# Out-projection of a linear-attention layer: seven feature blocks of the products first, the transposes one token block behind, the first feed-forward pair in column halves

## The chip, the core and the metric

One Trainium2 chip, one of its cores. The metric is the device time of one execution in microseconds (us); lower is better. TensorE (PE) multiplies, VectorE (DVE), ScalarE (ACT) and GpSimd (POOL) work on rows, and SP issues most of the loads. Line numbers such as L173 are those of the kernel before.

## What is computed

512 tokens of 1024 features go through two blocks and a third layer behind them. The change lies in the first block, between its linear attention (eight groups of 128 features) and its feed-forward. Cut to what matters:

```python
def rwkv7_out(y, ...):
    ...
    return ((yn + bonus) * gate) @ w_o            # yn: y normalised per head of 64; w_o: 1024 x 1024

def first_block(x, ...):                          # i = 0
    ...
    h = x * (1.0 + sc1) + sh1
    y = rwkv7_mixer(h, ...)                       # ends in rwkv7_out
    x = layer_norm(DN_ALPHA * x + gt1 * y, ln_g[i, 0], ln_b[i, 0])
    x = layer_norm(DN_ALPHA * x + gt2 * channel_mixer(x * (1.0 + sc2) + sh2), ln_g[i, 1], ln_b[i, 1])

def swiglu(h, w1, w3, w2):                        # the channel_mixer here, 2816 hidden features
    return (jax.nn.silu(h @ w1) * (h @ w3)) @ w2
```

The vectors sh1, sc1, gt1, sh2, sc2 and gt2 are products of a conditioning vector with a table `ada_w` (6144 columns for each block).

## The kernel before

Every large product is made three times: a matrix is split into a high part that TensorE takes exactly (a cast on ScalarE, L167) and a low part, the rest (a subtraction on VectorE, L168), and `mm3` (L173) sums high x high, high x low and low x high.

**Attention tail.** `tail(f)` normalises the attention output of feature group f, adds the bonus, multiplies by the gate and writes the 128 features x 512 tokens to DRAM, `ygd[f]`. Three of its row operations are on GpSimd (L909, L913 and the product with `rs`, L924).

**Out-projection** (in `body`, L2113 to L2142). The eight pieces of `ygd` are loaded into `xres`, split into the high and low part of y (`y3`, two of the three buffers of the pool `act`), and then `x` is loaded over them into `xres`. After that the loads and splits of `w_o` stand in the code. The loop goes over four blocks of 128 tokens; for each, two halves of 512 output features, each of 8 feature blocks x 3 = 24 products of 512 columns into one bank of PSUM, and `resid_add` (L1314 to L1318, two VectorE operations of 128 x 512: product with the gate, sum with `xres`). Then `norm_tail` normalises the block's rows and brings them into feature order: statistics on VectorE, three small steps on GpSimd (L1136 to L1138), the scaling on ScalarE (L1139), two row operations on GpSimd that write `xres` for later (L1148, L1149), eight transposes on TensorE (L1162), eight scaled copies out of PSUM, `u` (ScalarE L1169, VectorE L1171 in turns), and the split into the high and low part `hT` (L167, L168 "act<-u"). `hT` is allocated at the first block: its high part gets the third `act` buffer, its low part that of y's high part, so that the low part's first write waits for y's last reader.

**Feed-forward.** `phase_ffn` goes over pairs of 128 hidden features; `glu` makes for each feature 24 products with w1 and 24 with w3 over all 512 tokens. Weights come by `load_w` (L155) in pieces of 1 MB through the pool `w` (four buffers) and are split in `k.part`. After each feature the generator `side` takes a step of `ada_sum`: eight loads of `ada_w` (L283, 256 KB each, three slots) and a running sum over them on VectorE (L288, or ScalarE L285 and GpSimd L286 for a second table), and three steps later a sum over partitions on TensorE (L274). These slots and sums lie in `free`, the next `act` buffer, that of y's low part:

```python
free = tok()
nc.gpsimd.memset(free[:, 3], 0.0)
side = (x for g in (k.ada_sum(free, psp, sp, 0, a["ada_w"][1], a["ada_b"][1], "1", False), ...
block, room = phase_ffn(k, hT, xres, gate0, psp, sp, gp, act, side)
```

The order in which each engine takes its instructions is fixed at build time by a scheduler; each engine and each load queue then works in order.

Of the kernel before, what the change touches and what calls it, by code (L numbers as in the profile page):

```python
# [18 lines left out]
NT = 512  # L19
NCX = 256  # L20
NA = NT + NCX
KB = 8
# [98 lines left out]
def at(t, *ix):  # L121

    return t[0][ix], t[1][ix]
# [181 lines left out]
def phase_rwkv(k, tables, tables2, modulate, yg):  # L305
# [223 lines left out]
    with ExitStack() as eb:  # L529
# [372 lines left out]
        def tail(f):  # L902

            st = fst[f]
            y3 = st["ysb"]
            vtok = k.t(tp1, [128, 4, 128], tag="vtok")
            nc.sync.dma_start(out=vtok, in_=vd[0:NT, f * 128:(f + 1) * 128].rearrange("(b p) n -> p b n", p=128))
            vh = vtok.rearrange("p b (h v) -> p (b h) v", h=2)
            nc.gpsimd.tensor_tensor(out=vh, in0=vh, in1=st["cf"][:, :, None].to_broadcast([128, 8, 64]), op=OP.mult)  # L909
# [3 lines left out]
            nc.gpsimd.tensor_tensor(out=y3, in0=y3, in1=mean[:, :, None].to_broadcast([128, 8, 64]), op=OP.subtract)  # L913
# [10 lines left out]
            nc.gpsimd.tensor_tensor(out=y3, in0=y3, in1=rs[:, :, None].to_broadcast([128, 8, 64]), op=OP.mult)  # L924
# [217 lines left out]
def norm_tail(k, sp, psp, tb, xres, gbc, bbc, hT, scol, bcol):  # L1142
# [7 lines left out]
    if hT is not None:  # L1150
        to_feature(k, sp, psp, xh, hT, slice(tb * 128, (tb + 1) * 128), scol, bcol)
# [49 lines left out]
def glu(k, psp, sp, xT, n, w1, w3, g):  # L1201
# [3 lines left out]
    for i in range(w1.shape[2] // 128):  # L1205
        pss = []
        for w in (w1, w3):
# [52 lines left out]
def phase_ffn(k, hT, xres, gate2, psp, sp, gp, act, side):  # L1260
# [4 lines left out]
    for f0, f1 in FCH:  # L1265
# [5 lines left out]
        for f in range(f0, f1, 2):  # L1271
# [7 lines left out]
            with tc.issue_after(k.sums.ins) if k.sums is not None else nullcontext():  # L1279
                glu(k, psp, sp, hT, NT, w1, w3, out)  # L1280
# [774 lines left out]
def body(tc, a, out):  # L2055
    nc = tc.nc
    with ExitStack() as es:
# [45 lines left out]
        with ExitStack() as e1:  # L2103
# [9 lines left out]
            with tc.tile_pool(reuse_waits="tile", name="wo3", bufs=5) as wo3:  # L2113
                y3 = feat()

                yg = xres.rearrange("p t d -> p (t d)").rearrange("p (f n) -> p f n", f=KB)
                for f in range(KB):
                    nc.sync.dma_start(out=yg[:, f, :], in_=ygd[f])
                for f in range(KB):
                    k.part_to(*at(y3, ALL, f), yg[:, f, :])  # L2120
                nc.sync.dma_start(out=xres, in_=a["x"][0].rearrange("(t p) d -> p t d", p=128))
# [4 lines left out]
                hT = None  # L2126
                for tb in range(4):
                    for hf in range(2):
                        ps = k.t(psp, [128, 512], tag="mm")
                        for kk in range(KB):  # L2130
                            k.mm3(ps, at(y3, ALL, kk, slice(tb * 128, (tb + 1) * 128)), at(ws[hf * 4 + kk // 2], ALL, kk % 2), kk == 0, kk == KB - 1)
                        resid_add(k, sp, tb, hf, ps, gate, xres)
                    hT = hT or feat()
# [139 lines left out]
```

## Time and profile before

| | |
|---|---|
| median of 3 runs | 3027.36 us (3026.72 to 3030.48) |
| the profiled execution | 3030.04 us; span of the core 3028.3 us |
| mean granted TensorE clock | 0.903 |
| TensorE busy | 2658.0 us (88%) |
| VectorE, ScalarE, GpSimd busy | 1716.0 us (57%), 1333.8 us (44%), 825.0 us (27%) |
| memory read and written | 419.34 MB and 55.39 MB, 157 GB/s over the span |

Busy shares are means over some thirty different stages and say little about one of them. The places that the change touches lie between 1040 and 1330 us of the span.

### The profile page before, as it was taken

How to read it: one execution, taken by the hardware profiler on the slowest of the kernel's cores; microseconds unless marked ns; L12 is line 12 of the kernel's file. 1: busy time of each engine (PE TensorE's matmuls, PEld its weight loads, DVE VectorE, ACT ScalarE, POOL GpSimd, SP SyncE). 2: the span in 40 equal slices, each digit the busy share in tenths (PEclk: the TensorE clock that was granted, in tenths of full speed). 3: DMA queues.
4: the chain of work that ended last, by engine and by line, in shares of the span. 5: the costliest groups of instructions: out<-in, count | busy, mean ns of one | idle time of the engine just before them, and what ended most of it. 6: DMA issues, size and time to landing. Idle time of an engine off the chain costs nothing. (4 is left out here: it accounts for less than half of the span.)

```text
span 3028.3 us, 47973 instructions
## 1 busy us (share of the span) xinstructions
PE 2658.0 (88%) x18816; PEld 2001.1 (66%) x18816; DVE 1716.0 (57%) x2526; ACT 1333.8 (44%) x2338; POOL 825.0 (27%) x908
## 2 busy tenths in 40 slices
PE   5878788898898756989998999999958989989999
PEld 3666577677776545768776666455547845778887
DVE  5865566756655436664446323456676367554544
ACT  5644555555554423215452322345544377442422
POOL 2453434534534321016654300000023200112120
PEclk8976888997887867989998999999979989999999
DMA  7572344544543535666541877778662212122321
GB/s 257 182 222 66 96 125 142 181 137 129 172 133 95 186 129 165 222 189 212 186 150 63 306 258 271 258 258 287 233 239 88 68 43 74 56 84 94 102 90 64
DMA packets 301823, 477.92 MB, mean 158 GB/s; under 512 B 47282, under 2 KB 176067, under 8 KB 294935
## 3 DMA queue, kind: packets, MB, share of 16 engines
q1 hardware_dynamic: 283896, 404.81, 40.6%
q0 software_dynamic: 10480, 60.31, 6.0%
q10 hardware_dynamic: 7216, 9.68, 0.9%
q8 instruction: 150, 2.46, 0.3%
q14 instruction: 81, 0.66, 0.1%
HBM read 419.34 MB, written 55.39 MB: 157 GB/s over the span
## 5 line engine op out<-in xcount | busy, mean ns | idle before, releaser
L168 DVE TENSOR_TENSOR wl<-w,wh 128x1024 fp32r<-128x1024 f32 (+2 forms) x400 | 477.3, 1203 | 622.3 <-ACT wh L167 618.9
L167 ACT CAST wh<-w 128x1024 fp32r<-128x1024 f32 (+2 forms) x400 | 382.8, 966 | 636.4 <-PE mm L173 438.8
L173 PE MATMUL mm<-act,wh 128*128 128x512 f32 x1408 | 441.1, 395 | 18.6 <-ACT act L167 14.8
L173 PEld LDWEIGHTS mm<-act,wh 128*128 128x128 f32 x1408 | 266.8, 190 | 78.7 <-ACT act L167 15.4
L173 PE MATMUL mm<-wh,act 128*128 128x512 f32 x948 | 308.1, 402 | 7.8 <-ACT wh L167 4.5
L173 PE MATMUL mm<-act,wl 128*128 128x512 f32 x704 | 277.3, 394 | 4.5 <-DVE wl L168 4.5
L173 PEld LDWEIGHTS mm<-wh,act 128*128 128x128 f32 x948 | 182.4, 194 | 57.3 <-issue 7.8
L173 PE MATMUL mm<-wl,act 128*128 128x512 f32 x474 | 190.9, 403 | 0.1
L286 POOL TENSOR_TENSOR act<-act 128x512 f32<-128x512 f32 x96 | 145.3, 1513 | 152.8 <-ACT act L285 137.8
L301 POOL DMA_DIRECT2D bc<-gate x6 | 3.6, 592 | 619.2 <-DVEq L1730 516.3
L173 PEld LDWEIGHTS mm<-act,wl 128*128 128x128 f32 x704 | 133.6, 190 | 36.3 <-DVE wl L168 8.4
L799 DVE STREAM_TRANSPOSE XT<-T 128x512 f16<-128x512 f16 x120 | 84.6, 705 | 99.8 <-ACT T L797 99.7
L743 POOL TENSOR_TENSOR GA<-GA,masks 128x512 f32<-128x512 f32 (+1 forms) x96 | 100.2, 1053 | 102.8 <-ACT GA L742 99.6
L285 ACT ACTIVATE act<-act,cT 128x512 f32<-128x512 f32 x96 | 68.4, 724 | 118.4 <-DMA act<-in_w_ada_dram 117.7
L739 PE MATMUL gm<-kr,bk 64*128 64x128 f32 (+1 forms) x768 | 115.7, 327 | 3.8 <-ACT GA L742 2.0
L792 DVE TENSOR_TENSOR W<-pW,masks 128x512 f16<-128x512 f32 x120 | 81.8, 681 | 63.5 <-PE pW L790 59.7
L739 PEld LDWEIGHTS gm<-kr,bk 64*128 64x128 f32 x768 | 99.7, 226 | 24.5 <-ACT GA L742 9.3
L173 PE MATMUL mm<-wh,moxl 128*128 128x512 f32 (+1 forms) x336 | 113.9, 382 | 0.0
L173 PEld LDWEIGHTS mm<-wl,act 128*128 128x128 f32 x474 | 91.8, 194 | 31.1 <-DVE wl L168 5.0
L850 POOL TENSOR_TENSOR SP<-S,pc 128x64 f32<-128x64 f32 x176 | 58.3, 349 | 196.2 <-DVE S L890 184.8
L173 PE MATMUL mm<-wh,moxh 128*128 128x512 f32 (+1 forms) x336 | 107.3, 389 | 4.9 <-ACT wh L167 4.9
L797 ACT CAST T<-pT 128x512 f16<-128x512 f32 x120 | 69.6, 580 | 84.1 <-PE pT L795 80.9
(522 smaller groups left out, 6142.6 us busy)
## 6 DMA issues: line engine op xcount, KB each, us to landing
w<-in_moe_w_dram SPq DMA_DIRECT2D x136, 512.0 KB
w<-in_moe_w_dram SPq DMA_DIRECT2D x40, 1024.0 KB
w<-in_ffn_w_dram SPq DMA_DIRECT2D x32, 1024.0 KB
act<-in_ada_w_dram SPq DMA_DIRECT2D x96, 256.0 KB
act<-in_w_ada_dram SPq DMA_DIRECT2D x96, 256.0 KB
w<-in_moe_w_dram SPq DMA_DIRECT2D x64, 384.0 KB
w<-in_w_up_dram SPq DMA_DIRECT2D x22, 1024.0 KB
x<-xdk POOLq DMA_DIRECT2D x18, 1024.0 KB, 5.7
```

Of the source, the lines that this page charges most:

```text
L167: self.nc.scalar.copy(out=hi, in_=x)
L168: self.nc.vector.tensor_tensor(out=lo, in0=x, in1=hi.bitcast(F32), op=OP.subtract)
L173: self.nc.tensor.matmul(ps, x, y, start=start and i == 0, stop=stop and i == 2, skip_group_check=True)
L285: nc.scalar.activation(out=wt, in_=wt, func=AF.Copy, scale=c)
L286: nc.gpsimd.tensor_tensor(out=acc, in0=wt, in1=acc if kk else bias, op=OP.add)
L301: (eng or self.nc.gpsimd).dma_start(out=t, in_=row_ap.to_broadcast([128, D]))
L739: nc.tensor.matmul(pss[par][:, s2, d, :nc_], bkj(d, par, j), KR[d][PR(par), j::12, :][:, :nc_ // 64, :], start=True, stop=True)
L743: nc.gpsimd.tensor_tensor(out=out, in0=out, in1=gm, op=OP.mult)
L792: nc.vector.tensor_tensor(out=W16, in0=pW, in1=lmask[:, li, None].to_broadcast(sh), op=OP.mult)
L797: nc.scalar.copy(out=T16, in_=pT)
L799: nc.vector.transpose(fl(XT), fl(T16))
L850: nc.gpsimd.tensor_tensor(out=SP[:, d], in0=S[:, d], in1=PC[d][:, j:j + 1].to_broadcast([128, 64]), op=OP.mult)
```

## The change

The tail of the last group (f = 7) has its three row operations on VectorE. `w_o` is loaded and split first. y's high part takes one `act` buffer and its low part two buffers of the weight pool `w`; the eighth piece of `ygd` goes to a buffer of its own, so that x is loaded once the seventh is split. `hT` takes the two other `act` buffers, and `free` the one of y's high part.

The products of a token block are cut into feature blocks 0 to 6 and feature block 7. `norm(tb)` holds the last feature block, the residual and the normalised rows; `turn(tb)` the transposes, the copies and the split. They are written in the order of the last lines of the diff. The transposes of blocks 2 and 3 stand in the first feed-forward feature, which is made in two column halves.

```diff
@@ tail
+            eng = nc.gpsimd if f < 7 else nc.vector
...
-            nc.gpsimd.tensor_tensor(out=y3, in0=y3, in1=mean[:, :, None].to_broadcast([128, 8, 64]), op=OP.subtract)
+            eng.tensor_tensor(out=y3, in0=y3, in1=mean[:, :, None].to_broadcast([128, 8, 64]), op=OP.subtract)
...
@@ norm_tail
-def norm_tail(k, sp, psp, tb, xres, gbc, bbc, hT, scol, bcol):
+def norm_rows(k, sp, tb, xres, gbc, bbc):
...
-    if hT is not None:
-        to_feature(k, sp, psp, xh, hT, slice(tb * 128, (tb + 1) * 128), scol, bcol)
+    return xh
@@ glu
+        if cols is not None and i == 0:
+            ws = [k.part(w[:, :, :128]) for w in (w1, w3)]
+            pss = [k.t(psp, [128, 512], tag="mm") for _ in ws]
+            for cs, make in cols:
+                make()
+                for w, ps in zip(ws, pss):
+                    for kk in range(KB):
+                        k.mm3(ps[:, cs], at(w, ALL, kk), at(xT, ALL, kk, cs), kk == 0 and cs.start == 0, kk == KB - 1 and cs.stop == n)
+        for w in (w1, w3) if not pss else ():
...
@@ body
-                y3 = feat()
...
+                yh = k.t(act, [128, KB, NT], F32R, tag="act")
+                yl = [k.t(k.wp, [128, 4, NT], F32R, tag="w") for _ in range(2)]
...
+                y7 = k.t(sp, [128, 512], tag="silu")
                 for f in range(KB):
-                    nc.sync.dma_start(out=yg[:, f, :], in_=ygd[f])
+                    nc.sync.dma_start(out=yg[:, f, :] if f < 7 else y7, in_=ygd[f])
                 for f in range(KB):
-                    k.part_to(*at(y3, ALL, f), yg[:, f, :])
+                    k.part_to(yh[:, f], yl[f // 4][:, f % 4], yg[:, f, :] if f < 7 else y7)
+                    if f == 6:
+                        nc.sync.dma_start(out=xres, in_=a["x"][0].rearrange("(t p) d -> p t d", p=128))
...
+                hT = feat()
+                pss = {}
+
+                def products(tb, k0, k1):
                     for hf in range(2):
...
+                        if k0 == 0:
+                            pss[tb, hf] = k.t(psp, [128, 512], tag="mm")
+                        for kk in range(k0, k1):
+                            cs = slice(tb * 128, (tb + 1) * 128)
+                            k.mm3(pss[tb, hf], (yh[:, kk, cs], yl[kk // 4][:, kk % 4, cs]), at(ws[hf * 4 + kk // 2], ALL, kk % 2), kk == 0, kk == KB - 1)
...
+                def norm(tb):
+                    products(tb, 7, 8)
+                    for hf in range(2):
+                        resid_add(k, sp, tb, hf, pss[tb, hf], gate, xres)
+                    rows_[tb] = norm_rows(k, sp, tb, xres, *gb)
+
+                def turn(tb):
+                    to_feature(k, sp, psp, rows_[tb], hT, slice(tb * 128, (tb + 1) * 128), *cols)
+
+                products(0, 0, 7)
+                products(1, 0, 7)
+                norm(0)
+                products(2, 0, 7)
+                norm(1)
+                turn(0)
+                products(3, 0, 7)
+                norm(2)
+                turn(1)
+                norm(3)
+                turns = [(slice(0, 256), lambda: None), (slice(256, 512), lambda: (turn(2), turn(3)))]
...
-                block, room = phase_ffn(k, hT, xres, gate0, psp, sp, gp, act, side)
+                block, room = phase_ffn(k, hT, xres, gate0, psp, sp, gp, act, side, turns)
```

How the scheduler orders it is seen at three places. The names are tiles: mm is a bank of PSUM, token blocks are counted from 0, wh and wl are the high and low part of w_o (or of a feed-forward weight), act and u as above, rsq the normalised rows.

TensorE, before, from the end of token block 0 (mm_13870) to block 1 (mm_13939), with block 0's transposes (rsq_13900):

```order
L173 MATMUL mm_13870<-wh_13838,act_13775 128x512
L173 MATMUL mm_13870<-wl_13839,act_13775 128x512
L173 MATMUL mm_13870<-wh_13838,act_13776 128x512
L1162 MATMUL mm_13915<-ctile,rsq_13900 128x128 x4
L1162 MATMUL mm_13927<-ctile,rsq_13900 128x128 x4
L173 MATMUL mm_13939<-wh_13804,act_13775 128x512
L173 MATMUL mm_13939<-wl_13805,act_13775 128x512
L173 MATMUL mm_13939<-wh_13804,act_13776 128x512
```

TensorE, of the change, at block 0's transposes (rsq_13946); mm_13912 belongs to block 1, mm_13961 to block 2, mm_14056 to block 3:

```order
L173 MATMUL mm_13912<-wh_13811,act_13815 128x512
L173 MATMUL mm_13912<-wl_13812,act_13815 128x512
L173 MATMUL mm_13912<-wh_13811,w_13817 128x512
L173 MATMUL mm_13961<-wh_13791,act_13815 128x512
L173 MATMUL mm_13961<-wl_13792,act_13815 128x512
L1162 MATMUL mm_14032<-ctile,rsq_13946 128x128 x4
L1162 MATMUL mm_14044<-ctile,rsq_13946 128x128 x4
L173 MATMUL mm_14056<-wh_13777,act_13815 128x512
L173 MATMUL mm_14056<-wl_13778,act_13815 128x512
L173 MATMUL mm_14056<-wh_13777,w_13816 128x512
```

Before, block 0's transposes stand between its last product and block 1's first one; now they stand in block 2's last feature block, and all products of block 1 and nearly all of block 2 lie ahead of them.

VectorE, before, behind block 3's first half (bnst_14186 its statistics, silu_14182 the gate product of its second half; act_13899 is hT's low part, which waits for y's last reader; wl_14248, wl_14277 and wl_14331 belong to the first feed-forward features):

```order
L1130 BN_STATS bnst_14186<-xres 128x6
L1381 CAST rt_b_16909<-rt_ct 128x128
L168 TENSOR_TENSOR wl_14248<-w_14242,wh_14247 128x1024
L168 TENSOR_TENSOR act_13899<-u_13920,act_13898 128x4x128
L168 TENSOR_TENSOR act_13899<-u_13932,act_13898 128x4x128
L168 TENSOR_TENSOR wl_14277<-w_14244,wh_14276 128x1024
L1314 TENSOR_TENSOR silu_14182<-mm_14157,bc_13761 128x512
L168 TENSOR_TENSOR wl_14331<-w_14242,wh_14330 128x1024
L1171 TENSOR_SCALAR u_14015<-mm_14010,fs0a,fo0a 128x128
```

VectorE, of the change, from block 3's first product with the gate (silu_14157; silu_14160 is its second half, bnst_14113 and bnag_14116 are block 2's statistics, act_13845 is hT's low part of block 1, act_14190 a step of the table):

```order
L1323 TENSOR_TENSOR silu_14157<-mm_14056,bc_13761 128x512
L1390 CAST rt_b_16959<-rt_ct 128x128
L1171 TENSOR_SCALAR u_14132<-mm_14127,fs0a,fo0a 128x128
L1131 BN_STATS bnst_14113<-xres 128x6
L1323 TENSOR_TENSOR silu_14160<-mm_14078,bc_13761 128x512
L168 TENSOR_TENSOR wl_14381<-w_14196,wh_14380 128x1024
L1171 TENSOR_SCALAR u_14144<-mm_14139,fs0a,fo0a 128x128
L288 SCALAR_TENSOR_TENSOR act_14190<-act_14190,cT 128x512
L1327 SCALAR_TENSOR_TENSOR xres<-xres,silu_14157 128x512
L1133 BN_AGGR bnag_14116<-bnst_14113 128x2
L168 TENSOR_TENSOR act_13845<-u_14132,act_13844 128x4x128
```

Operations of blocks 1, 2 and 3, a weight split and a step of the table now stand among each other, ahead of the low part of block 1; the list before has no step of the table at this place.

GpSimd, of the change, from block 1's last row operation on (bnrs_14120 is block 2, bnrs_14171 block 3, rsq_14112 block 2):

```order
L1150 TENSOR_TENSOR xres<-xres,bb_13765 128x1024
L2177 MEMSET act_14190 128x1024
L1137 TENSOR_SCALAR bnrs_14120<-bnag_14116 128x1
L1138 TENSOR_TENSOR bnrs_14120<-bnrs_14120,mhalf 128x1
L1139 TENSOR_TENSOR bnrs_14120<-bnrs_14120,bnnm_14118 128x1
L1137 TENSOR_SCALAR bnrs_14171<-bnag_14167 128x1
L1149 TENSOR_TENSOR xres<-rsq_14112,bg_13763 128x1024
L1138 TENSOR_TENSOR bnrs_14171<-bnrs_14171,mhalf 128x1
L1150 TENSOR_TENSOR xres<-xres,bb_13765 128x1024
L1139 TENSOR_TENSOR bnrs_14171<-bnrs_14171,bnnm_14169 128x1
```

The same place before (block 2 is bnrs_14098 and rsq_14090, block 3 bnrs_14193):

```order
L1136 TENSOR_SCALAR bnrs_14098<-bnag_14094 128x1
L1137 TENSOR_TENSOR bnrs_14098<-bnrs_14098,mhalf 128x1
L1138 TENSOR_TENSOR bnrs_14098<-bnrs_14098,bnnm_14096 128x1
L1148 TENSOR_TENSOR xres<-rsq_14090,bg_13763 128x1024
L1149 TENSOR_TENSOR xres<-xres,bb_13765 128x1024
L2140 MEMSET act_14236 128x1024
L1136 TENSOR_SCALAR bnrs_14193<-bnag_14189 128x1
L1137 TENSOR_TENSOR bnrs_14193<-bnrs_14193,mhalf 128x1
L1138 TENSOR_TENSOR bnrs_14193<-bnrs_14193,bnnm_14191 128x1
```

Block 3's three small steps followed each other before, behind block 2's two row operations of 128 x 1024; now those two stand between them.

On SP's queue the four first feed-forward loads stood ahead of the loads of `ygd`; now two of them stand behind those and ahead of x, and the other two behind x and between the first loads of the table.

## Rows read from the trace of the kernel before

**Rows 1.** TensorE timeline: start, us, line, out<-in, xcount, idle before and its releaser

```profile
1083.90 0.79 PE L173 MATMUL mm<-wh,act 128*128 128x512 f32 x1 [3.25 <-ACT act L167]
...
1107.31 1.97 PE L1162 MATMUL mm<-ctile,rsq 128*128 128x128 f32 x8 [9.16 <-ACT rsq L1139]
...
1125.84 1.97 PE L1162 MATMUL mm<-ctile,rsq 128*128 128x128 f32 x8 [4.98 <-ACT rsq L1139]
...
1131.73 0.62 PE L173 MATMUL mm<-wh,act 128*128 128x512 f32 x2
...
1132.41 0.62 PE L173 MATMUL mm<-wh,act 128*128 128x512 f32 x2
...
1158.27 0.39 PE L173 MATMUL mm<-wh,act 128*128 128x512 f32 x1
1170.74 1.97 PE L1162 MATMUL mm<-ctile,rsq 128*128 128x128 f32 x8 [12.09 <-ACT rsq L1139]
...
1183.60 0.80 PE L173 MATMUL mm<-act,wh 128*128 128x512 f32 x1 [1.94 <-DVE act L168]
```

**Rows 2.** Stretches: us, busy PE, PEld, DVE, ACT, POOL, granted clock, DMA, GB/s

```profile
1083.90:1089.90 6.00, 6.00 (x13) 4.30 (x14) 3.61 (x6) 3.37 (x6) 0.00 (x0) 0.50 0.84 285
1183.60:1189.20 5.60, 5.60 (x13) 4.46 (x14) 3.89 (x6) 0.00 (x0) 0.00 (x0) 0.51 0.63 188
```

**Rows 3.** VectorE timeline, 1100 to 1187 us

```profile
1100.92 0.69 DVE L1318 SCALAR_TENSOR_TENSOR xres<-xres,silu 128x512 f32<-128x512 f32 x1 [4.99 <-DMA xres<-in_x_dram]
...
1108.95 0.41 DVE L1171 TENSOR_SCALAR u<-mm,fs0a,fo0a 128x128 f32<-128x128 f32 x1 [4.14 <-ACT u L1169]
...
1157.06 1.22 DVE L168 TENSOR_TENSOR wl<-w,wh 128x1024 fp32r<-128x1024 f32 x1 [1.52 <-ACT wh L167]
1158.47 1.29 DVE L168 TENSOR_TENSOR act<-u,act 128x512 fp32r<-128x512 f32 x2 [0.18 <-PE mm L173]
...
1171.62 2.05 DVE L288 SCALAR_TENSOR_TENSOR act<-act,cT 128x512 f32<-128x512 f32 x1
1173.92 3.10 DVE L168 TENSOR_TENSOR act<-u,act 128x512 fp32r<-128x512 f32 x2
...
1182.20 0.75 DVE L288 SCALAR_TENSOR_TENSOR act<-act,cT 128x512 f32<-128x512 f32 x1 [2.57 <-DMA act<-in_ada_w_dram]
...
1184.07 2.41 DVE L288 SCALAR_TENSOR_TENSOR act<-act,cT 128x512 f32<-128x512 f32 x3
```

**Rows 4.** TensorE timeline, 1260 to 1330 us

```profile
1289.31 1.87 PE L274 MATMUL mm<-ctile,act 128*128 128x2 f32 x8 [9.46 <-DVE act L288]
...
1302.55 1.84 PE L274 MATMUL mm<-ctile,act 128*128 128x2 f32 x8 [11.37 <-DVE act L288]
```

**Rows 5.** GpSimd timeline, 1040 to 1200 us

```profile
1069.59 1.04 POOL L913 TENSOR_TENSOR yc<-yc,gnm 128x512 f32<-128x512 f32 x1 [17.18 <-DVE gnm L912]
...
1170.78 2.35 POOL L1148 TENSOR_TENSOR xres<-rsq,bg 128x1024 f32<-128x1024 f32 x1 [0.76 <-ACT rsq L1139]
```

**Rows 6.** SP's queue, 1040 to 1200 us: issue, us to issue all, line, load

```profile
1062.99 6.26 SPq L155 DMA_DIRECT2D w<-in_ffn_w_dram  x4
...
1091.65 0.38 SPq L2121 DMA_DIRECT2D xres<-in_x_dram  x1
...
1158.73 1.28 SPq L283 DMA_DIRECT2D act<-in_ada_w_dram  x3
```

**Rows 7.** SP's queue, 1227 to 1258 us (between: two feed-forward loads, eight table loads)

```profile
1227.79 10.37 SPq L283 DMA_DIRECT2D act<-in_ada_w_dram  x8
...
1257.78 10.49 SPq L283 DMA_DIRECT2D act<-in_ada_w_dram  x8
```

**Rows 8.** TensorE timeline, products of 256 columns at full clock, 321 us

```profile
320.96 0.28 PE L979 MATMUL bg<-wl,x 128*128 128x256 f32 x1
...
321.31 0.28 PE L979 MATMUL bg<-wl,x 128*128 128x256 f32 x1
```

**Rows 9.** ScalarE timeline, 1100 to 1180 us

```profile
1144.03 1.24 ACT L1139 ACTIVATE rsq<-xres,bnrs 128x1024 f32<-128x1024 f32 x1 [18.25 <-POOL bnrs L1138]
```

More of the change, by code (lines that the diff above doesn't have):

```diff
@@ L908, in tail @@
             vh = vtok.rearrange("p b (h v) -> p (b h) v", h=2)
-            nc.gpsimd.tensor_tensor(out=vh, in0=vh, in1=st["cf"][:, :, None].to_broadcast([128, 8, 64]), op=OP.mult)
+            eng.tensor_tensor(out=vh, in0=vh, in1=st["cf"][:, :, None].to_broadcast([128, 8, 64]), op=OP.mult)
             mean = k.t(tp, [128, 8], tag="gnm")
@@ L923, in tail @@
             nc.gpsimd.tensor_tensor(out=rs, in0=var, in1=hp_, op=OP.pow)
-            nc.gpsimd.tensor_tensor(out=y3, in0=y3, in1=rs[:, :, None].to_broadcast([128, 8, 64]), op=OP.mult)
+            eng.tensor_tensor(out=y3, in0=y3, in1=rs[:, :, None].to_broadcast([128, 8, 64]), op=OP.mult)
             g2 = k.t(tp1, [128, 128], tag="g2")
@@ L1257, with phase_ffn @@
 TB = (0, 128, 256, 384)
-def phase_ffn(k, hT, xres, gate2, psp, sp, gp, act, side):
+def phase_ffn(k, hT, xres, gate2, psp, sp, gp, act, side, cols):
     tc, nc, a = k.tc, k.nc, k.a
@@ L1279, in phase_ffn @@
             with tc.issue_after(k.sums.ins) if k.sums is not None else nullcontext():
-                glu(k, psp, sp, hT, NT, w1, w3, out)
+                glu(k, psp, sp, hT, NT, w1, w3, out, cols if f == 0 else None)
         add = lambda tb, hf, ps: resid_add(k, sp, tb, hf, ps, gate2, xres, ALPHA if f0 == 0 else None)
@@ L2113, in body @@
             with tc.tile_pool(reuse_waits="tile", name="wo3", bufs=5) as wo3:
-                y3 = feat()
-                yg = xres.rearrange("p t d -> p (t d)").rearrange("p (f n) -> p f n", f=KB)
-                for f in range(KB):
-                    nc.sync.dma_start(out=yg[:, f, :], in_=ygd[f])
-                for f in range(KB):
-                    k.part_to(*at(y3, ALL, f), yg[:, f, :])
-                nc.sync.dma_start(out=xres, in_=a["x"][0].rearrange("(t p) d -> p t d", p=128))
                 ws = []
@@ L2125, in body @@
                     ws += [k.part(raw[:, 2 * q:2 * q + 2, :], wo3 if len(ws) + q < 5 else k.wq) for q in range(2)]
-                hT = None
-                for tb in range(4):
-                    for hf in range(2):
[L2129 to L2133, printed above, removed]
-                    norm_tail(k, sp, psp, tb, xres, *gb, hT, *cols)
+                yh = k.t(act, [128, KB, NT], F32R, tag="act")
@@ new lines, in body @@
+                yl = [k.t(k.wp, [128, 4, NT], F32R, tag="w") for _ in range(2)]
+                yg = xres.rearrange("p t d -> p (t d)").rearrange("p (f n) -> p f n", f=KB)
+                y7 = k.t(sp, [128, 512], tag="silu")
+                for f in range(KB):
+                    nc.sync.dma_start(out=yg[:, f, :] if f < 7 else y7, in_=ygd[f])
+                for f in range(KB):
+                    k.part_to(yh[:, f], yl[f // 4][:, f % 4], yg[:, f, :] if f < 7 else y7)
+                    if f == 6:
+                        nc.sync.dma_start(out=xres, in_=a["x"][0].rearrange("(t p) d -> p t d", p=128))
@@ new lines, in body @@
+                rows_ = {}
+                def norm(tb):
[8 more added lines that the diff above has]
+                norm(0)
```

3 lines of the change are left out of this document (1 added, 2 removed).

## The prediction

> **What bounds the kernel now.** I read the timeline of TensorE around the out-projection first, then the stretches with the granted clock, then the same microseconds on VectorE, GpSimd and the load queue, and last the place behind it where TensorE waits next.
>
> TensorE computes the out-projection in token blocks, and between two blocks it stands still. The reader is to see three bracketed waits in [rows 1] that the normalisation L1139 releases: 9.16 us behind block 0, 4.98 behind block 1 (behind block 2 about the same again) and 12.09 after the last product at 1158.27; and then, from the transposes at 1170.74, another 12.9 us until 1183.60, when the feed-forward's products start to flow. That is because transposes stand ahead of the next block's products in TensorE's order: while block 0 is normalised, block 1's products sit behind transposes that can't start. From the first product (1083.90) to the end of the last (1158.27 + 0.39) 74.8 us go by. The waits cost twice: after them the clock stands at its lower level (0.50 of full speed in the two stretches of [rows 2]), and there a product takes 0.427 us instead of 0.227 (three products from 1131.73 to 1132.41 are 0.68 us, [rows 1]; at half the clock twice that, less a little, taken as 0.427). In the first 6.0 us, at half clock, the profile has 13 products [rows 2]; I count 14.
>
> The last part has a second cause. Two `act` buffers hold the attention output y and only one is left, so the low part of the transposed blocks waits for the last product: L168 act<-u runs at 1158.47, 0.18 us after it [rows 3]. The transposed blocks 0, 1 and 2 are finished only then, queued with everything else.
>
> Further on TensorE stands still again, 9.46 us before 1289.31 and 11.37 us before 1302.55, for L288, VectorE's running sum over `ada_w` (the table stream) [rows 4]. A gain on TensorE that the table stream doesn't make too is lost there. So the change is worth the smaller of two shifts: that of TensorE and that of the stream.
>
> **The change, part by part.** I count t from the first product, so before's last product ends at t = 74.8.
>
> Tail of group 7. Two row operations move from GpSimd (1.04 us, [rows 5]) to VectorE, where a 128x512 operation takes 0.69 [rows 3]; both lie on the chain to the last `ygd` write. 2 x 0.35 = 0.7 us earlier. The third (vtok) moves off the path and costs 0.69 us of an idle VectorE: nothing.
>
> Products. There are 192 (4 blocks x 2 halves x 8 feature blocks x 3) and now nothing stands between them that isn't ready. Block 0's transposes come after 138 products and two more: 14 x 0.427 + 126 x 0.227 = 34.6. Block 0's products are complete after 94: 24.2. From there the chain to the transposes is 4.98 (TensorE's wait behind block 1 [rows 1], which is this chain for one half) plus 2.1 for three operations of the other half, 0.69 each, so ready at 31.3, 3 us before they are reached. Block 1's are reached at about 46; its products end at 34.2, and 7.1 plus four u operations of block 0 between them puts it at about 43. So no wait. The 16 transposes of two blocks take 1.97 per 8 at half clock [rows 1], 2.0 for all at full clock. Last product: 6.0 + 178 x 0.227 + 2.0 = **48.4 instead of 74.8, 26.4 us earlier.** If both slacks of 3 us were lost it would be 20; more than 26.4 has no source.
>
> x has to be there at 24 to 28. It is issued when the seventh block is split, about as before (1091.65, [rows 6]), and its first user waited 4.99 us, until 1100.92 [rows 3]: 9.3 us for 2 MB. Two feed-forward loads now stand ahead of it on SP's queue. Their price: from 1227.79 to 1257.78 sixteen table loads and two feed-forward loads go out in 30.0 us, where eight table loads alone take 10.4 [rows 7], so two feed-forward loads cost 9.2. At worst x lands at 1110.1, t = 26.2; the chain behind it has 3 us of slack. I take nothing.
>
> Behind the last product. This is where I expect less than it looks. VectorE works in order; between block 2's first product with the gate and the low part that the feed-forward's first half needs there stand 20 operations (10 of 0.69, two weight splits of 1.22, four u of 0.41 and a table step of 0.75 [rows 3], three small ones of some 0.2): 12.4 us, from 46 to about 58. TensorE waits some 9.5 us. Then 48 products of 256 columns: three take 0.35 us at the full clock [rows 8], so 0.117 each and 0.213 at half; half and half, 7.9 us, to 66. Splitting into columns costs 96 x 0.117 against 48 x 0.227, 0.3 us: nothing. Block 3's normalisation meanwhile needs nine more VectorE operations (4.8 us, to 63) and then GpSimd, whose order now puts block 2's two row operations (2.35 for one, [rows 5]) between block 3's small steps: 69. With the normalisation's 1.24 us [rows 9] block 3's transposes start at about 70, 22 us after the last product instead of 12. From there to flowing products before took 12.9 us, of which a wait for a table load (2.57 ahead of 1182.20) and slow operations are part [rows 3]; eight operations in turn on two engines and a split are 6 at least. I take 8: 78. The second half's 48 products end the pair at 86. Before, the pair's 48 products ended 13.4 us after 1183.60 (13 in 5.6 at half clock [rows 2], 35 x 0.227), t = 113.1. **TensorE gains 27**, so the column halves give 1 of it and the products 26; bounds 22 (12.9 instead of 8) and 29.
>
> GpSimd slows VectorE there: beside its row operation at 1170.78 a table step took 2.05, where three took 2.41 together, and two low parts 3.10 instead of the 1.29 of 1158.47 [rows 3]. I count one such meeting, 1.3 to 2 us, and it is in the 8. The Trainium skill, GPSIMD Engine Reference, section Specifications, says that GpSimd shares its SBUF interfaces with VectorE, with contention for VectorE instructions of two SBUF inputs. The trace agrees as to these rows; by that rule every table step between t = 63 and 75 would meet a row operation, and the gain would be that of rival 2.
>
> The table stream. Its buffer is now y's, free at the last product: first load at 48.4 instead of 74.8 (1158.73, [rows 6]). The low parts of block 3 stand behind the eleventh and twelfth step; before, the twelfth ended at 1186.48 [rows 3], t = 102.6, now about 79. **The stream gains 23.6**; bounds 18 and 26, since the second pair's second feed-forward load (before issued at 1062.99, in an idle queue [rows 6]) now goes out beside it at 4.6 us.
>
> Sum: 0.7 + 23.6 = 24.3 earlier, carried to 1302.55 by the stream and by TensorE after it. The profiled execution took 3030.04, so 3005.7; the median of the runs shown is 2.7 lower, and 3027.36 - 24.3 = **3003**.
>
> **Rivals.**
> 1. The stream doesn't hold TensorE and all of its shift survives. For: VectorE waits for loads in that stretch in only some of the steps. Against: two waits of 20.8 us together [rows 4]. 0.7 + 27 to 29: 2998 to 3000. Chance 0.12.
> 2. Contention eats a third. The loads that moved into the stream's start (9.2 for two) or seven table steps 1.3 slower each (9.1). Gain about 15: 3012. For: both prices are measured. Against: three loads were in flight when the stream was slowest before, too. Chance 0.20.
> 3. The gain is given back further on, by an engine that I haven't found to wait. Within 6 us of 3027. Against: everything behind 1302.55 starts from TensorE's and the stream's ends. Chance 0.05.
> 4. Slower: the stream starts no earlier, because y's buffer is released late, and pays 9.2 for the loads that came from the idle queue: 3036. It decides if the first table load goes out later than 1158.73 - 9.2, t = 65.6. Against: the last product stands at 48.4 and its slacks are 3 us. Chance 0.05.
>
> **How the numbers follow.** My forecast has 0.58, and its own range is 2999 to 3008 (gain 19 to 28). With rival 1 and most of rival 2 the range is 2995 to 3015, which leaves out about 0.17. 0.2% is 6 us, about what a measurement of this kernel tells from no change. Faster: 0.58 + 0.12 + 0.20 = 0.90; same 0.05; slower 0.05.
>
> **What would show it.** TensorE without a wait over 1 us from the first product to the last, and that within 47 to 52 us; x's user not waiting; one wait of 8 to 11 us behind the last product and another ahead of block 3's transposes; a first table load 25 to 27 us earlier than before; waits for L288 further on that are no shorter than before. Wrong would be: a wait ahead of the transposes of block 0 or 1 (the slack of 3 us), x landing after t = 28, or a stream whose twelfth step is less than 18 us earlier.

## The result, and the profile after

The changed kernel takes 2997.06 us (median of 4 runs, 2995.27 to 2997.87), the kernel before 3028.65 us on the same chip (4 runs, 3026.72 to 3030.48). The ratio is 0.9897, with a 95% interval of 0.9882 to 0.9912: about 31 us faster. The forecast was 3003, 2995 to 3015; the likeliest case alone had 2999 to 3008, and the time is just below that. The time lies in the range; the single steps were off, in both directions.

The stretches of both profiled executions, cut at the first product, at the end of the first feed-forward feature, at the last sum that TensorE waits for, and at the first pooling product, which opens the stage behind the feed-forward (columns as in [rows 2]). A row has the line numbers of its own kernel: L1140 is the normalisation L1139. Before:

```profile
0.00:1083.90 1083.90, 897.28 (x10853) 701.34 (x10854) 675.26 (x1004) 561.75 (x1179) 461.95 (x626) 0.83 0.49 154
1083.90:1197.10 113.20, 72.68 (x275) 58.03 (x276) 54.89 (x90) 28.96 (x44) 26.44 (x24) 0.76 0.36 117
1197.10:1302.55 105.45, 84.61 (x388) 68.79 (x386) 70.30 (x100) 24.35 (x32) 0.53 (x1) 0.92 0.67 219
1302.55:1604.60 302.05, 293.42 (x1272) 233.90 (x1273) 157.31 (x168) 132.52 (x179) 154.70 (x106) 0.98 0.55 175
1604.60:3028.30 1423.70, 1309.96 (x6032) 939.06 (x6030) 758.26 (x1165) 586.25 (x905) 181.38 (x152) 0.95 0.45 156
```

and after:

```profile
0.00:1081.68 1081.68, 897.47 (x10853) 699.92 (x10854) 677.93 (x1008) 562.09 (x1180) 459.73 (x623) 0.83 0.48 150
1081.68:1171.00 89.32, 67.22 (x322) 57.55 (x322) 50.41 (x85) 27.16 (x42) 28.09 (x24) 0.82 0.59 189
1171.00:1279.42 108.42, 85.48 (x389) 69.03 (x388) 73.31 (x104) 26.36 (x34) 0.53 (x1) 0.91 0.67 216
1279.42:1577.50 298.08, 290.88 (x1272) 232.45 (x1273) 156.80 (x168) 132.70 (x179) 153.43 (x106) 0.99 0.56 177
1577.50:2993.50 1416.00, 1303.92 (x6032) 939.71 (x6030) 758.93 (x1165) 586.78 (x905) 180.83 (x152) 0.95 0.46 157
```

The gains are 2.2, 23.9, -3.0, 4.0 and 7.7 us, 34.8 in these two executions (3030.04 and 2995.27 us). The stretch that the change touches gives 23.9 and three of them are lost at the next place, as forecast. Nearly 10 us come from the first and the last stretch, where the prediction had only the 0.7 of the tail, and the rest of their code is the same.

TensorE's timeline after, which answers to [rows 1]:

```profile
1081.68 0.79 PE L173 MATMUL mm<-wh,act 128*128 128x512 f32 x1 [3.30 <-ACT act L167]
...
1115.58 1.03 PE L1162 MATMUL mm<-ctile,rsq 128*128 128x128 f32 x8
...
1126.94 1.03 PE L1162 MATMUL mm<-ctile,rsq 128*128 128x128 f32 x8
...
1128.97 0.40 PE L173 MATMUL mm<-wh,w 128*128 128x512 f32 x1
1134.75 0.80 PE L173 MATMUL mm<-act,wh 128*128 128x256 f32 x2 [5.38 <-ACT act L167]
1138.68 0.58 PE L173 MATMUL mm<-act,wh 128*128 128x256 f32 x1 [3.13 <-DVE act L168]
...
1146.64 1.04 PE L1162 MATMUL mm<-ctile,rsq 128*128 128x128 f32 x8
1150.00 1.20 PE L1162 MATMUL mm<-ctile,rsq 128*128 128x128 f32 x8 [2.32 <-ACT rsq L1140]
1162.47 1.51 PE L173 MATMUL mm<-act,wh 128*128 128x256 f32 x4 [11.26 <-ACT act L167]
```

Between the first product and the last there is no bracket any more, and the transposes of blocks 0 and 1 take 1.03 us instead of 1.97. Behind the last product there are 5.38 + 3.13 us of waiting, then the first column half, then 11.26 us ahead of the second half. On VectorE the same microseconds read, from the first table step to the twelfth:

```profile
1136.61 0.73 DVE L288 SCALAR_TENSOR_TENSOR act<-act,cT 128x512 f32<-128x512 f32 x1
...
1147.16 3.04 DVE L288 SCALAR_TENSOR_TENSOR act<-act,cT 128x512 f32<-128x512 f32 x3 [4.45 <-DMA act<-in_ada_w_dram]
1150.12 0.40 DVE L1171 TENSOR_SCALAR u<-mm,fs0a,fo0a 128x128 f32<-128x128 f32 x1
1151.48 1.47 DVE L288 SCALAR_TENSOR_TENSOR act<-act,cT 128x512 f32<-128x512 f32 x1 [0.96 <-DMA act<-in_ada_w_dram]
1152.87 0.40 DVE L1171 TENSOR_SCALAR u<-mm,fs0a,fo0a 128x128 f32<-128x128 f32 x1
1154.13 1.56 DVE L288 SCALAR_TENSOR_TENSOR act<-act,cT 128x512 f32<-128x512 f32 x1 [0.86 <-DMA act<-in_ada_w_dram]
1155.62 0.72 DVE L1171 TENSOR_SCALAR u<-mm,fs0a,fo0a 128x128 f32<-128x128 f32 x2
...
1163.26 0.75 DVE L288 SCALAR_TENSOR_TENSOR act<-act,cT 128x512 f32<-128x512 f32 x1
```

Block 2's copies u of 0.4 us each stand one by one behind table steps, and these wait for their loads: from 1146.64 to 1155.62 VectorE has made two copies. The load queue and the next waits for the table, which answer to [rows 6] and [rows 4]:

```profile
1129.17 0.82 SPq L283 DMA_DIRECT2D act<-in_ada_w_dram  x2
...
1132.01 4.76 SPq L155 DMA_DIRECT2D w<-in_ffn_w_dram  x2
...
1139.91 19.10 SPq L283 DMA_DIRECT2D act<-in_ada_w_dram  x8
```

```profile
1265.13 1.87 PE L274 MATMUL mm<-ctile,act 128*128 128x2 f32 x8 [8.41 <-DVE act L288]
...
1279.42 0.77 PE L274 MATMUL mm<-ctile,act 128*128 128x2 f32 x3 [12.42 <-DVE act L288]
```

The table starts 29.6 us earlier than before, right behind the last product; the eight loads behind its first four take 19.10 us (16.49 before); and TensorE waits for L288 as long as it did (20.8 us in the two rows, both times).

### The profile page after: what moved, and what is told of

It is laid out like the page before. It is cut to its first block, busy times and chain, and to the rows that moved or that the text cites. A ratio compares the mean times of both kernels' runs of the same rounds, so it can differ in the third digit from the quotient of the medians.

```text
span 2993.5 us, 48068 instructions
## 1 busy us (share of the span) xinstructions
PE 2645.0 (88%) x18864; PEld 1998.6 (67%) x18864; DVE 1717.4 (57%) x2529; ACT 1335.1 (45%) x2338; POOL 822.6 (27%) x905
## 5 line engine op out<-in xcount | busy, mean ns | idle before, releaser
L173 PE MATMUL mm<-act,wh 128*128 128x512 f32 (+1 forms) x1440 | 446.1, 392 | 28.7 <-ACT act L167 22.8
L173 PEld LDWEIGHTS mm<-act,wh 128*128 128x128 f32 x1440 | 273.3, 193 | 87.5 <-ACT act L167 23.8
L173 PE MATMUL mm<-wh,act 128*128 128x512 f32 x884 | 288.1, 398 | 7.2 <-ACT wh L167 3.9
L173 PE MATMUL mm<-act,wl 128*128 128x512 f32 (+1 forms) x720 | 280.8, 390 | 4.8 <-DVE wl L168 4.8
L173 PEld LDWEIGHTS mm<-wh,act 128*128 128x128 f32 x884 | 168.1, 191 | 51.6 <-ACT wh L167 6.1
L285 ACT ACTIVATE act<-act,cT 128x512 f32<-128x512 f32 x96 | 68.4, 724 | 112.1 <-DMA act<-in_w_ada_dram 111.8
L288 DVE SCALAR_TENSOR_TENSOR act<-act,cT 128x512 f32<-128x512 f32 x96 | 74.2, 773 | 57.8 <-DMA act<-in_ada_w_dram 56.8
```

Of the source, the lines that this page charges most:

```text
L173: self.nc.tensor.matmul(ps, x, y, start=start and i == 0, stop=stop and i == 2, skip_group_check=True)
L285: nc.scalar.activation(out=wt, in_=wt, func=AF.Copy, scale=c)
L288: nc.vector.scalar_tensor_tensor(out=acc, in0=wt, scalar=c, in1=acc if kk else bias, op0=OP.mult, op1=OP.add)
```

## The experiments

From here t is again microseconds from the first product of the out-projection. Each line is one profile: differences of start times in the timelines, except the last column.

| kernel | first product at | last product | first table load | first feature done | last sum waited for | first pooling product | pooling to end |
|---|---|---|---|---|---|---|---|
| before | 1083.9 | 74.4 | 74.8 | 113 | 218.7 | 520.7 | 1423.7 |
| changed | 1081.7 | 47.3 | 47.5 | 89 | 197.7 | 495.8 | 1416.0 |
| changed, again (e9) | 1079.7 | 48.0 | 48.2 | 89 | 198.4 | 496.0 | 1417.7 |
| e1 tail alone | 1079.4 | 74.8 | 75.3 | 113 | 219.1 | 519.2 | 1429.6 |
| e2 no column halves | 1088.1 | 47.7 | 47.9 | 95 | 201.5 | 502.3 | 1424.2 |
| e3 order of before | 1081.0 | 77.2 | 77.4 | 104 | 221.2 | 524.1 | 1420.9 |
| e4 four slots, three sums | 1077.8 | 46.9 | 47.1 | 89 | 351.9 | 498.2 | 1419.2 |
| e5 step held | 1082.3 | 46.6 | 46.8 | 81 | 201.9 | 502.2 | 1418.9 |
| e6 four slots, four sums | 1077.1 | 47.9 | 48.1 | 90 | 180.2 | 474.6 | 1418.7 |
| e7 no loads, changed | 1081.2 | 47.4 | 47.6 | 99 | none | 477.7 | - |
| e8 no loads, before | 1080.1 | 75.4 | 75.9 | 122 | none | 498.4 | - |
| e10 e6 and e5 | 1075.8 | 47.0 | 47.2 | 82 | 185.0 | 477.5 | 1423.7 |
| e11 splits of w_o late | 1066.5 | 47.7 | 47.9 | 90 | 193.0 | 493.7 | 1415.7 |
| e12 e10 and e11 | 1068.8 | 47.4 | 47.6 | 82 | 183.0 | 477.5 | 1417.7 |

The whole times scatter far more here than in the first comparison (26 runs of the kernel before went from 3012.67 to 3048.30 us), so the readings rest on the columns up to the first pooling product. There the two profiles of the changed kernel differ by 0.2 us (by up to 0.7 in the columns before it), and those of before and e1, whose code is the same from the first product on, by 1.5. Smaller differences in that column tell nothing.

**e1: the tail alone.** The kernel before, with only the first hunk of the change.

> The kernel before with only the last tail's three row operations moved to VectorE. My theory (two row operations of 1.04 us become 0.69 each on the chain to the last write of y, nothing else): 0.7 to 0.8 us faster than before, about 3027.8, and the stretch from the last copy of y to the first product shorter by 0.7. Rival (the whole 2.2 us by which the first product came earlier in the changed kernel belong to the tail): 2.2 us faster. In both, the stretches behind the feed-forward are those of the kernel before, so this profile also shows how much of the 8.5 us that the changed kernel gained behind its second wait for the table is the luck of one profile: if its TensorE clock between the feed-forward's end and the router is again below 1.00, the dip belongs to the kernel before, and not to one execution.

Measured 3029.45 against 3029.49 us, ratio 1.0001 (0.9977 to 1.0025): too little for whole times to tell. In the traces, from the copy of y (ScalarE L899) to the tail's last row operation, it is 12.91 us before (1067.78 to 1080.69), and 12.04 both here (1064.09 to 1076.13) and in the changed kernel (1066.38 to 1078.42): the tail is worth 0.87. The rival falls. The dip of TensorE's granted clock behind the feed-forward: from the first pooling product to the first product of the router (tile rt_w) it takes 24.6 us before, 23.0 here with the same code; so the dip belongs to the execution.

**e2: no column halves.**

```diff
-                turns = [(slice(0, 256), lambda: None), (slice(256, 512), lambda: (turn(2), turn(3)))]
+                turn(2)
+                turn(3)
+                turns = None
```

> The changed kernel without the column halves: transposes of blocks 2 and 3 stand ahead of the first feed-forward pair, which is made over all 512 columns. By the prediction's working (the pair ends at 86 with halves, the halves give 1 us) the pair ends 1 us later and the time is 0 to 2 us above that of the changed kernel, 2997 to 2999. Rival, from the changed kernel's trace, where the first half's 48 products took about 12 us while block 3 was being normalised: all 48 products of 512 columns then stand behind block 3, some 6 to 8 us later, but since the table stream holds TensorE further on the time still rises by less than 3 us. A rise of 6 or more would say that the pair's end, and not the stream, carries the gain.

3011.11 us, ratio 0.9936 (0.9904 to 0.9968), where the changed kernel has 0.9897 (0.9882 to 0.9912). TensorE's timeline:

```profile
1149.67 1.97 PE L1162 MATMUL mm<-ctile,rsq 128*128 128x128 f32 x8 [13.44 <-ACT rsq L1140]
1158.89 1.97 PE L1162 MATMUL mm<-ctile,rsq 128*128 128x128 f32 x8 [7.25 <-ACT rsq L1140]
1166.72 1.65 PE L173 MATMUL mm<-act,wh 128*128 128x512 f32 x3 [5.86 <-ACT act L167]
1170.97 0.80 PE L173 MATMUL mm<-act,wh 128*128 128x512 f32 x1 [2.60 <-DVE act L168]
```

The first feature is done 6 us later, the last waited sum comes 3.8 us later, the first pooling product 6.5 later. The halves are worth some 4 to 6 us: they fill the 13.44 us in which block 2 is normalised. By what I had written, a rise of 6 says that the pair's end carries the gain; e5 was made to separate the two.

**e3: the buffers alone.**

```diff
-                products(0, 0, 7)
...
-                turns = [(slice(0, 256), lambda: None), (slice(256, 512), lambda: (turn(2), turn(3)))]
+                for tb in range(4):
+                    products(tb, 0, 7)
+                    norm(tb)
+                    turn(tb)
+                turns = None
```

> The changed kernel's buffers, loads and tail, but the products in the order of before: all eight feature blocks of a token block, its rows, its transposes, then the next block; no column halves. Theory (the products' order gives the gain): the waits between token blocks come back, 9 and 5 and 5 us, the last product stands near t = 72 from the first, the first table load goes out then, and the time is 15 to 25 us above that of the changed kernel, 3012 to 3022. Rival (the buffers give the gain, since the low part no longer waits for the last product): within 8 us of the changed kernel, 2997 to 3005.

3031.0 us, ratio 1.0006 (0.9979 to 1.0034): nothing is left of the gain, where I had expected 15 to 25 us to go.

```profile
1105.09 1.97 PE L1162 MATMUL mm<-ctile,rsq 128*128 128x128 f32 x8 [11.48 <-ACT rsq L1140]
...
1124.37 1.97 PE L1162 MATMUL mm<-ctile,rsq 128*128 128x128 f32 x8 [5.92 <-ACT rsq L1140]
...
1169.02 1.97 PE L1162 MATMUL mm<-ctile,rsq 128*128 128x128 f32 x8 [10.51 <-ACT rsq L1140]
```

The waits of before are back. The low parts no longer wait for the last product, and the first feature ends 9 us earlier than before, but the first table load goes out at 77.4, and the end of the feed-forward is not earlier (524.1 for 520.7).

**e4 and e6: four slots for the table.** e4 takes the fourth slot from the running sums, e6 from a new buffer for the bias row. The lines of e6:

```diff
-        ws, accs, (bias,) = ([room[...] ...] for o, m in ((0, 3), (3, 4), (7, 1)))
+        ws, accs = ([room[...] ...] for o, m in ((0, 4), (4, 4)))
...
-                wt, c = ws[kk % 3], self.cT[:, kk, row:row + 1]
+                wt, c = ws[kk % 4], self.cT[:, kk, row:row + 1]
...
+                bias = k.t(gp, [128, 512], tag="bias")
```

> The changed kernel with four slots for table loads instead of three and three running sums instead of four (sums over partitions two steps later instead of three). Theory (the table stream, with three loads in flight, holds TensorE at the two waits of 8.4 and 12.4 us): a step takes less than 1.3 us, the two waits shrink by more than half, and the time falls by 8 to 18 us, to 2979 to 2989. Rival (memory or VectorE bounds the stream, or the earlier sums take it back): within 4 us of the changed kernel. If the stream doesn't hold TensorE at all, rival 1 of the prediction, also no change.

> The changed kernel with four slots for table loads and still four running sums; the bias row lies in a buffer of its own. In the run with four slots and three sums the stream was 10.8 us faster at its 48th step and 31 us at the 96th, but the end of the feed-forward came at 498.2 us from the first product against 495.8, with a new wait of 13.7 us at a sum of the second table. Theory (the stream holds TensorE; there the sums, needed a step earlier, took the gain back): the waits for L288, 21 us together in the changed kernel, fall below 8, no new wait over 5 us comes, and the end of the feed-forward stands at 480 to 489; the time 7 to 15 us below the changed kernel's. Rival (the stream's speed is not what holds TensorE): 494 to 499 again, time within 4 us of the changed kernel's.

e4: 2997.97 us, ratio 0.9904 (0.9869 to 0.9940), no gain. What TensorE waits for in it, from the first product to the pooling (us in total, times, longest), decides nothing yet:

```profile
PE mm L274 <- DVE act L288: 14.8, 3, 9.6
PE mm L274 <- POOL act L286: 13.7, 1, 13.7
...
PE mm L268 <- POOL act L286: 4.1, 1, 4.1
```

The first table's waits shrank from 21.1 to 14.8, and 17.8 us of new ones came from the second table, whose sums now stand one step nearer to their adds. e6, with the sums where they were: 2979.77 us, ratio 0.9842 (0.9800 to 0.9883), and

```profile
PE mm L274 <- DVE act L288: 6.3, 1, 6.3
```

with no new row above 5 us but the one ahead of the second half (9.1, as 11.26 before). The first pooling product comes 21 us earlier than in the changed kernel. The stream does hold TensorE.

**e5: the first table step held back.**

```diff
...
-                    next(side, None)
+                    with tc.issue_after(k.low.ins) if f + i == 0 else nullcontext():   # k.low: last low part of hT
+                        next(side, None)
```

> The changed kernel with the first table step (eight L288) held on VectorE behind the last low part of blocks 2 and 3; its loads go out as before. In the changed kernel four of these steps, which wait for table loads, stand between the copies u of blocks 2 and 3, and the pair ends 89.3 us after the first product. Theory (these steps hold the transposed blocks, and the stream carries the gain further on): the pair ends 5 to 8 us earlier, at 81 to 84, the stream's twelfth step comes later than 82.3, and so the end of the feed-forward (first pooling product, 495.8 us after the first product in the changed kernel) does not come earlier than 493. Rival (the pair's end carries the gain): the end of the feed-forward comes 5 to 8 us earlier, 488 to 491. Rival 2 (the wait of 11.3 us is the copies' own chain of two engines): the pair's end moves by less than 2 us.

3006.77 us, ratio 0.9935 (0.9909 to 0.9962).

```profile
1145.80 1.91 PE L1162 MATMUL mm<-ctile,rsq 128*128 128x128 f32 x16
...
1154.88 1.43 PE L173 MATMUL mm<-act,wh 128*128 128x256 f32 x4 [7.17 <-ACT act L167]
```

The first feature is done at 81 instead of 89. About half of these 8 us lies between the transposes of block 3 and the products: 12.5 us in the changed kernel, some 8.1 here (estimated, with block 3's transposes as the second half of the row of 16). The other half lies ahead of them: block 3's rows are normalised at t = 61.8 instead of 67.0 and its transposes no longer wait. There e5 changed more than the table steps, since one row operation of GpSimd instead of two now stands among block 3's small steps. The first pooling product comes 6.4 us later all the same: a feature that is done earlier while the stream starts later loses. That answers e2's question: the pair's end alone doesn't carry the gain, and in e2 the table's steps came later too (the waited sums by 4.5 and 3.8 us).

**e7 and e8: the loads left out, in both kernels.**

```diff
+                if on_pool or i == 0 and kk < 3:
-                nc.sync.dma_start(out=wt, in_=w[kk * 128:(kk + 1) * 128, c0:c0 + n])
+                    nc.sync.dma_start(out=wt, in_=w[kk * 128:(kk + 1) * 128, c0:c0 + n])
```

> The changed kernel with all loads of the first table left out but the first three (the sums are taken over these three blocks again and again, so the modulation of the second block is not the reference's). VectorE's steps stay. Theory (the stream is the bound of that stretch): the waits of 8.4 and 12.4 us vanish, and the end of the feed-forward comes 15 to 25 us earlier than in the changed kernel, 470 to 481 us from the first product. Rival 1 of the prediction (it doesn't hold): less than 5 us. The copies u of blocks 2 and 3 then meet no step that waits for a load: the pair should end at 83 to 86 instead of 89.3.

> The kernel before with the same loads left out (the same part of the result is not the reference's). Against the run before this one it gives the change's worth when no stream limits it, that is TensorE's own shift. By the prediction's working 27 at the first pair and 27 at the end of the feed-forward (with the table 23.4 to 24.9 were measured): end of the feed-forward 497 to 508. Rival (the change's worth is set by TensorE alone and the table adds a constant to both): the difference between the two is that with the table, 23 to 25.

Later stages run on other data here, so their whole times (4877.41 and 4900.23 us) say nothing. In both the wait for L288 is gone. The first pooling product comes 18 us earlier in the changed kernel (477.7) and 22 in the one before (498.4): the waits were the loads', not VectorE's. The change alone, with no stream, is worth 20.7 us there and 22.5 at the first feature: less than with the table, and not the 27 of the prediction. The copies did not get their 83 to 86: without loads the scheduler puts more table steps ahead of them, and these run beside GpSimd's row operations (four of 2.4 to 2.8 us between 1142.83 and 1156.25),

```profile
1142.82 13.97 DVE L289 SCALAR_TENSOR_TENSOR act<-act,cT 128x512 f32<-128x512 f32 x8
```

```profile
1169.55 1.23 PE L173 MATMUL mm<-act,wh 128*128 128x256 f32 x3 [16.89 <-ACT act L167]
```

and the second half waits 16.89 us. Eight steps in a row took 1.75 us each there, where a step alone takes 0.74 (L289 at 1138.75): 8.0 us more. So e7 does not tell what the steps cost in the changed kernel, and that TensorE's own shift is larger than the stream's doesn't follow from it.

**e9: the changed kernel once more.**

> The changed kernel once more. Seven profiles of kernels that share all code behind the feed-forward gave 1416.0 (the changed kernel) to 1429.6 us from the first pooling product to the end, and 1423.7 in the kernel before; the first product came 1077 to 1088 us after the start in kernels that share the code ahead of it but for the tail. Theory (forecast right at the end of the feed-forward, 23 to 25 us; the other 7 of the 31.6 us belong to executions): the end of the feed-forward again at 495 to 498 us from the first product, but the rest again somewhere between 1416 and 1430, so that it lies mostly above 1416; the median 22 to 30 us below that of before. Rival (the changed kernel's own timing shortens the stages behind it): 1416 to 1418 again, and 30 to 33 us below.

2997.65 us against 3023.08, ratio 0.9909 (0.9889 to 0.9928), about 27.5 us (22 to 34), as the theory had it. The first pooling product repeats within 0.2 us; behind it 1417.7, by the number the rival. That stretch, of one and the same code, took 1415.7 to 1429.6 us in twelve profiles, the three with the old order 1420.9 to 1429.6, the nine with the new one 1415.7 to 1424.2: the means are 5.6 us apart and the ranges overlap. In all twelve it holds the same 6032 instructions of TensorE, busy for 1301.7 to 1315.1 us, and what is left is 112.1 to 116.4. Of the 7.7 us between before and after, 6.0 are busy time (1309.96 and 1303.92 in the rows above), so it is hardly a wait that got shorter. It stays open whether a few microseconds there belong to the change.

**e10, e11, e12: towards a better version.** e10 is e6 with e5's hold. In e11 the casts of w_o wait on ScalarE for the last tail:

```diff
+                    with tc.issue_after(k.hold[i // 2].ins):      # the tail's square, then its last scaled copy
...
```

> The run with four slots and four sums, and with the first table step held on VectorE behind the low parts of blocks 2 and 3 as in the run that held it alone. There the pair ended 8.3 us earlier and the feed-forward 6.4 us later, because the stream came late. Theory (with four slots the stream has 10 us to spare at its 48th step, so holding it costs less than the pair's 8 us gain): end of the feed-forward 468 to 473 us from the first product, against 474.6 with the slots alone. Rival (the stream is still the bound, one wait of 6.3 us was left): 476 to 482.

> The changed kernel with the splits of w_o held on ScalarE behind the last tail (the first four casts behind its square, the last four behind its scaled copies). In the kernels before and after, eight casts that wait for loads of w_o stand ahead of the last attention chunk's copies on ScalarE, and TensorE waits 8.42 and 7.71 us for them at 1061 us. Theory: those waits fall below 2 us, the first product of the out-projection comes 6 to 10 us earlier against 1081.1 (the mean of eight profiles), 1071 to 1075, and the order behind it is unchanged (end of the feed-forward 495 to 498 us from the first product). Rival (the casts then stand in the tail's way, and the loads of the eight pieces of y are next): less than 3 us.

> All three together: four slots and four sums, the first table step held, the splits of w_o behind the last tail. If each keeps what it gave: 6 to 10 us at the first product, 21 at the slots, 2 to 6 at the hold, that is 2960 to 2970 where the changed kernel has 2997. If the hold gives nothing, 2968 to 2975.

e10: 2983.13 us, ratio 0.9861 (0.9837 to 0.9884), first pooling product at 477.5: the rival; with four slots the hold still costs some 3 us, by one profile of each. e11: 2986.63, ratio 0.9884 (0.9857 to 0.9912); its first product comes at 1066.47, 9 us and more ahead of all but e12. The two rows that say why are ScalarE's and TensorE's in the changed kernel:

```profile
1058.12 1.99 ACT L167 CAST wh<-w 128x1024 fp32r<-128x1024 f32 x2 [5.32 <-DMA w<-in_rk_w_o_dram]
```

```profile
1060.33 0.69 PE L833 MATMUL ch<-Rs,TF 64*64 64x64 f32 x8 [7.71 <-ACT Rs L863]
```

A cast that waits for w_o stood ahead of the last attention chunk's copy; in e11 that bracket is 0.41. e12, with all three: 2970.83 us (2965.81 to 2979.02), ratio 0.9825 (0.9802 to 0.9848), the fastest here. Four slots and e11 without the hold, which by the table should be some 3 us better still (an estimate), was not run.

## Why the prediction was right, and where not

**Tail.** 0.7 forecast, 0.87 measured. The other 1.4 us by which the first product came earlier lie in a scatter of 1075.8 to 1088.1 over profiles that share all code ahead of it but for the tail.

**Products.** Right to a microsecond: no wait, transposes at 33.9 and 45.3 (34.6 and 46), last product done at 47.7 (48.4). x is there: its first user (VectorE L1327, 1105.96) has no bracket. e3 shows that this order is what the gain needs.

**Behind the last product.** The first part held: 8.5 us of waiting for 9.5, first half from t = 57.0 (58) to 65 (66), block 3's transposes at 68.3 (70). The step that failed is "eight operations in turn on two engines and a split are 6 at least. I take 8". It took 12.5, because the copies alternate with table steps that wait for loads; with these steps out of the way, in e5, it takes the forecast's 8. I had counted one meeting with GpSimd and none with the load queue. The Trainium skill, GPSIMD Engine Reference, section Specifications, has GpSimd share its SBUF interfaces with VectorE. The trace agrees: beside GpSimd's row operations five table steps took 3.04 + 1.47 + 1.56, where five alone take 3.7, so 2.4 us, a little above the 1.3 to 2 that I gave it. TensorE's shift was 23.9 instead of 27, inside the bounds (22 to 29).

**Column halves.** "So the column halves give 1 of it" failed as well: some 4 to 6 (e2). Without them all 48 products stand behind block 3, and the wait for block 2 is empty; I had set the halves' 7.9 us of products against nothing.

**Stream.** Its start is right (47.5 for 48.4). Its twelfth step ends at 82.3 instead of 79, a number that had no sum of its own behind it. From the end of the first step to that of the twelfth it is 26.7 us, where before, from the row below to 1186.48 [rows 3], it was 21.6: the moved feed-forward loads stand among the table's, as the lower bound (18) had it, and the steps beside GpSimd are in it too. The shift is 20.3 for 23.6, and 20.9 at the last sum that TensorE waits for (20.3 in e9). That the stream holds the end of the feed-forward is shown from three sides: e5 (feature 8 us earlier, end later), e6 (one more slot, 21 us) and e7 (no loads, no waits).

```profile
1164.14 0.75 DVE L288 SCALAR_TENSOR_TENSOR act<-act,cT 128x512 f32<-128x512 f32 x1 [0.27 <-DMA act<-in_ada_b_dram]
```

**Sum and rivals.** 23.6 were forecast for 1302.55, the last sum that TensorE waits for, and from there on; 20.9 came there. At the end of the feed-forward 24.9 and 24.7 were measured against the profile of before, 23.4 and 23.2 against e1. The 4.0 us in between have no term: 2.5 of them are TensorE's busy time for the same 1272 instructions (293.42 and 290.88), the rest are short waits, and the stretch takes 300.2 to 302.9 us in the three profiles with the old order and 297.6 to 300.9 in the five with the new order and three slots. That the sum is met so closely there is in part luck. The 34.8 us between the two profiles are 24.9, 2.2 ahead of the first product and 7.7 behind the pooling; of the last two the sum contained 0.7. So rival 1 (2998 to 3000) nearly has the time and is wrong as a mechanism, by e6. Rival 2's prices were real and smaller: 5.1 us over the twelve steps, with the 2.4 beside GpSimd among them, and no run parts the two. Without waits for loads, in e7, eight steps cost 8.0 us more, near the 9.1 that it had for seven. Rivals 3 and 4 did not come.

## What to carry to other kernels

Where a kernel waits twice, for a stage and for a stream of loads behind it, work out the shift of both, and test the claim by making the stream faster: here one more slot of 256 KB moved the end of the feed-forward by 21 us, the whole reordering by 23 to 25. Before a small chain is costed at its own operations, look at what its in-order engine holds between them, and whether that waits for memory. And compare two profiles stage by stage from a common event: up to the end of the changed stage profiles of the same code agreed within 0.2 us in one pair and 1.5 in another, while whole times of one kernel moved by 36.

## What the runs showed of the hardware

One code gave different times from one execution to the next far from the change. From the first pooling product to the end it took 1415.7 to 1429.6 us. Part of it is the granted clock. From the first pooling product to the router's first, the kernel before, the changed kernel and the changed kernel again:

```profile
1604.60:1629.18 24.58, 22.13 (x109) 18.45 (x107) 15.43 (x25) 5.46 (x6) 11.31 (x14) 0.93 0.06 22
```

```profile
1577.52:1600.48 22.96, 20.46 (x109) 17.31 (x107) 15.49 (x25) 5.48 (x6) 11.11 (x14) 1.00 0.08 24
```

```profile
1575.64:1600.25 24.61, 22.13 (x109) 18.45 (x107) 15.46 (x25) 5.48 (x6) 11.31 (x14) 0.93 0.06 22
```

109 instructions of TensorE each time, and 1.6 us between a clock of 0.93 and one of 1.00; the second and third row are the same program.

Loads of 256 KB did not keep one pace: with three slots the 96 loads of the first table take some 188 us (1129.17 to 1316.9), with four some 162 (1125.17 to 1286.7), at a mean DMA share of 0.69 and 0.77. The share rose with the fourth slot, so with three the stream was held by its slots more than by the memory.
